# Nine instead of eight of 22 pairs by Strassen's products in the down projection of a decoder block, with repacked operands, per-phase pools and delayed first loads

## The chip, the core and the metric

The kernel runs on one core of one Trainium2 chip. The core has a matrix engine (TensorE, PE in the profile), a vector engine (VectorE, DVE), a scalar engine (ScalarE, ACT), GpSimd (POOL) and SyncE (SP), which here issues nearly all transfers. Each engine has its own instruction stream, and engines wait for one another by semaphores. The metric is the time of one launch on the device in microseconds; lower is better.

## The reference

One layer of a decoder block, on 256 tokens of width 2048, in float32:

```
proj = x @ w_in                      # q, k, v, gates of two mixers
y_gla = gated linear attention -> @ w_branch_gla
y_fox = forgetting attention   -> @ w_branch_fox
x = layer_norm(ALPHA*x + (sigmoid(ma)*y_gla + sigmoid(mb)*y_fox) @ w_out)
h = gelu(causal_dwconv(x @ w_gate)) * (x @ w_up)     # 256 x 5632
x = layer_norm(ALPHA*x + h @ w_down)                 # the down projection
x = x + sigmoid(x @ w_ple_gate) * (p @ w_ple_proj)   # the last stage
```

The change concerns above all `h @ w_down`, a product of 256 x 5632 by 5632 x 2048, and on the side the start (the values `fv` of forgetting attention), the turn into the MLP after the first LayerNorm, and the last stage.

## The kernel before, in words

**Precision.** Every float32 operand is split in two parts of a shorter format: `hi`, a copy by ScalarE (helper `copy`, L84), and `lo = value - hi`, by VectorE (L150). A product is three matmuls, hi by hi, hi by lo and lo by hi, added up in a PSUM bank.

**Weights.** The weights lie in memory as units of 128 x 2048, in the order in which they are used. `prep` (L137) loads a unit in two halves of 128 x 1024 on SP's queue into `raw` (5 buffers), and splits each half into `hi` and `lo` (6 buffers each). `unit` (L156) hands out the next unit and prepares up to two units ahead. SP's stream has the order in which the program was written; ScalarE's and VectorE's orders are made by a scheduler; TensorE's order is as written in some stretches (the ends of the two LayerNorm stages).

**Stages in order of time:** `fv` (4 to 54 us) in eight units of weights of 128 x 2096 (`fv_prep` L325, matmuls L358), the other projections, the mixers, the output projection `wo` with the first LayerNorm (767 to 875), gate and up (`psg`, `psu`, until 1358.8), the down projection in two halves of 1024 columns, `dn0` (1358.8 to 1476) and `dn1` (to 1593), the second LayerNorm, and the last stage `pg0` and `pg1` (1599 to 1692) with its results (`ev_o`, L1208 to L1219). The program ends at 1697.2.

**The down projection.** The 5632 rows of `w_down` make 44 tiles of 128, taken as 22 pairs. For a pair and a half of the columns, 256 tokens by 256 rows by 1024 columns is a 2 x 2 by 2 x 2 block product. A classic pair does the eight block products, three matmuls of 512 columns each (`classic`, L1075, 24 matmuls). A Strassen pair does seven block products on sums and differences of blocks (`strassen`, L1085, matmuls at L1071, 21 matmuls); `fold` adds the extra banks into the result. `DN_S` names the pairs done so, `DN_ORDER` their order in each half. The sums of the left operand are made once, in gate and up, by `sums` (L964), for the pairs in `DN_Y` not before all gate and up matmuls are issued. The differences of the weights are made for every unit by `prep_s` (L115): it loads two halves, takes four differences `T` of 512 columns (L132) and splits seven operands, the 512-column pieces by `pair512` (L104, low parts at L111), one half whole (L126).

**Left operands** lie in tiles `hC` (two classic pairs' hi and lo) and `hS` (the seven operands of a Strassen pair). Small work tiles of 512 columns come from `t2` (L74): six buffers in the pool `sm`, for the whole kernel; the differences, the `sums`, `tho` and `res` of the last stage are among them.

**First LayerNorm.** `end1` (L878) transposes the normalised rows in four column groups per 128 tokens (`turn0`, `turn1`, PE L789) and weaves them into the first matmuls of gate and up: `phase0` does the first 128 tokens of three banks, `phase1(j)` the second 128 tokens of column group j (24 matmuls of 256 columns). `turn1(G[3])` comes behind `phase1(0)`. `begin2` (L1169) does the like for the second LayerNorm and `pg0`.

**The last stage.** `ev_o` takes a bank of 128 x 512: ScalarE's tanh into `tho`, VectorE's product into `tho` (L1215) and sum into `res` (L1217), and a store by SP (L1219).

**The start.** The first transfers on SP are the activations `xraw` (`load_x`, L166) and the `fv` weights `fvraw`. Unit 0 comes in three chunks per half; then units 1, the next activations and unit 2 are issued as soon as buffers allow.

Of the kernel before, what the change touches and what calls it, by code (L numbers as in the profile page):

```python
# [19 lines left out]
P = 128  # L20
# [12 lines left out]
NS = 1048  # L33
# [8 lines left out]
DN_ORDER = ((0, 1, 2, 4, 3, 6, 5, 9, 7, 8, 11, 10, 14, 12, 16, 13, 19, 15, 17, 18, 20, 21),  # L42
            (0, 1, 2, 4, 3, 6, 5, 9, 7, 11, 8, 14, 10, 16, 12, 19, 13, 15, 17, 18, 20, 21))
# [10 lines left out]
def tile_block(ctx: ExitStack, tc: tile.TileContext, wu, wfv, wpp, xT_in, x_in, pT_in, wlr,  # L54
# [7 lines left out]
    early = ctx.enter_context(ExitStack())  # L62
    ec = early.enter_context(tc.tile_pool(name="ec", bufs=1))
    pmm = ctx.enter_context(tc.tile_pool(name="pmm", bufs=6, space=PSUM))
# [9 lines left out]
    def t2(name):  # L74
        return sm.tile([P, 512], F32, tag="t2", bufs=6, name=name)
# [28 lines left out]
    def pair512(a, b, name):  # L104

        hi, lo = [ring.tile([P, 1024], F32R, tag=t, name=f"{t}{name}") for t in ("hi", "lo")]
        out = []
        for src, e in ((a, slice(0, 512)), (b, slice(512, 1024))):
            if src is not None:
                copy(hi[:, e], src)  # L110
                nc.vector.tensor_tensor(lo[:, e], src, hi[:, e].bitcast(F32), ALU.subtract)  # L111
                out.append((hi[:, e], lo[:, e]))
        return out

    def prep_s(u):  # L115

        r0, r1 = [ring.tile([P, 1024], F32, tag="raw", bufs=5, name=f"raw{u}_{h}")
                  for h in range(2)]
        for h, r in enumerate((r0, r1)):
            nc.sync.dma_start(r, wu[u, :, h * 1024:(h + 1) * 1024])  # L120
        b12, b11, b22, b21 = r0[:, 0:512], r0[:, 512:1024], r1[:, 0:512], r1[:, 512:1024]
        ops = pair512(b11, None, f"b11_{u}")
        hi = ring.tile([P, 1024], F32R, tag="hi", name=f"hi{u}_1")
        copy(hi, r1)
        lo = ring.tile([P, 1024], F32R, tag="lo", name=f"lo{u}_1")
        nc.vector.tensor_tensor(lo, r1, hi.bitcast(F32), ALU.subtract)  # L126
        ops += [(hi[:, 512:1024], lo[:, 512:1024]), (hi[:, 0:512], lo[:, 0:512])]
        ts = {}
        for n, a, b in (("T1", b12, b11), ("T3", b12, b22), ("T2", b22, "T1"),
                        ("T4", b21, "T2")):  # L130
            ts[n] = t2(f"{n}_{u}")
            nc.vector.tensor_tensor(ts[n], a, ts.get(b, b) if isinstance(b, str) else b,  # L132
                                    ALU.subtract)
        ops += pair512(ts["T1"], ts["T3"], f"t13_{u}") + pair512(ts["T2"], ts["T4"], f"t24_{u}")
        ready[u] = ops
# [203 lines left out]

    load_x(0, 0, 1, 1)  # L340
    f0 = fv_prep(0, (0,))
    load_x(0, 1, 2, 1)
# [3 lines left out]
    load_x(1, 0, 4)  # L346
    for u in range(8):
        hi, lo = fvu[u]
        for j in range(2):
            kt = 2 * u + j  # L350
            a = xT[kt // 4][:, kt % 4, :]
            for cs in ((0,), (1,), (2,)) if u == 0 else ((0, 1, 2),):
                for t in range(2):
                    ah, al = a[:, t * P:t * P + P], a[:, 256 + t * P:256 + t * P + P]
                    for i, (w, x) in enumerate(((hi[j], ah), (lo[j], ah), (hi[j], al))):
                        for c in cs:
                            o, n = fch[c]
                            nc.tensor.matmul(fbk[t][c][:, 0:n], lhsT=x, rhs=w[:, o:o + n],  # L358
                                             start=kt == 0 and i == 0,
                                             stop=kt == 15 and i == 2)  # L360
# [207 lines left out]
    def a_gen():  # L568
        it = 0
        for h in range(H):  # L570
# [8 lines left out]
            phl = sm.tile([P, 2, 2, P], F32R, tag="t2", bufs=6, name="phl")  # L579
# [74 lines left out]
    def o_gen():  # L654
        parts, ogs = {}, {}

        def split(h):
            vs = s8([P, 2, 2, 512], F32R, name=f"vs{h}")
            copy(vs[:, 0], vg[h][:, 0])
            nc.vector.tensor_tensor(vs[:, 1], vg[h][:, 0], vs[:, 0].bitcast(F32), ALU.subtract)  # L660
            ah, al = [sm.tile([P, 384], F32R, tag="t2", bufs=6, name=n) for n in ("ath", "atl")]
# [65 lines left out]
    late = ctx.enter_context(tc.tile_pool(name="late", bufs=1))  # L727

# [149 lines left out]
    def end1(tail_mm):  # L878
# [3 lines left out]
        with tc.manual_schedule(engines={mybir.EngineType.PE}):  # L882
# [76 lines left out]
    gp = [late.tile([P, 264], F32, name=f"gp{i}") for i in range(2)]  # L959
    for i in range(2):  # L960
        nc.gpsimd.memset(gp[i][:, 0:2], 0.0)
    hC, hS, hY, yps = {}, {}, [], {}

    def sums(y, pair):  # L964
# [3 lines left out]
        o = hS[pair] = s8([P, 7, 256], F32R, name=f"hS{pair}")  # L968
# [3 lines left out]
        for e, src in ((slice(0, 1), y[:, 0:1, 0:P]),  # L972
                       (slice(1, 3), y[:, 1, :].rearrange("p (t n) -> p t n", t=2)),
                       (slice(3, 7), v)):
            copy(o[:, e, 0:P], src)
            nc.vector.tensor_tensor(o[:, e, P:256], src, o[:, e, 0:P].bitcast(F32),
                                    ALU.subtract)
# [9 lines left out]
    for n in range(NF):  # L987
# [29 lines left out]
        else:  # L1017
            nc.vector.tensor_tensor(y, y, u, ALU.mult)
            i = DN_C.index(pair)
            if i % 2 == 0 and j == 0:  # L1020
                hC[i // 2] = (s8 if i < 12 else late.tile)([P, 4, 512], F32R,
                                                           name=f"hC{i // 2}")
            dst = hC[i // 2][:, i % 2 * 2 + j, :]
            copy(dst[:, 0:256], y)
            nc.vector.tensor_tensor(dst[:, 256:512], y, dst[:, 0:256].bitcast(F32),
                                    ALU.subtract)
        if n >= 4:
            pull(1)

    for pair in DN_Y:  # L1030
        sums(yps.pop(pair), pair)
# [19 lines left out]
    def down(nh, tail, mid):  # L1051
# [23 lines left out]
        def classic(pair, w, toks=(0, 1), cs=(0, 1)):  # L1075
            i = DN_C.index(pair)
            for j in range(2):
                a = hC[i // 2][:, i % 2 * 2 + j, :]
                for t in toks:
                    ah, al = a[:, t * P:t * P + P], a[:, 256 + t * P:256 + t * P + P]  # L1080
                    for x, v in ((ah, w[0][j]), (ah, w[1][j]), (al, w[0][j])):
                        for c in cs:
                            mm(C[t][c], x, v[:, c * 512:c * 512 + 512])

        def strassen(pair, ops):  # L1085
            for ps, i, (hi, lo) in zip(prods, left, ops):
                ah, al = hS[pair][:, i, 0:P], hS[pair][:, i, P:256]
# [154 lines left out]
def _dst(w):  # L1242

    out = []
    for nh in range(2):
        for n in DN_ORDER[nh]:
# [3 lines left out]
            out.append(np.concatenate([b[0][1], b[0][0], b[1][1], b[1][0]] if n in DN_S  # L1250
# [72 lines left out]
```

## Time and profile before

| what | us |
|---|---|
| median of three runs | 1697.54 (1697.37 to 1697.68) |
| profiled execution, its own time | 1699.05 |
| its span in the trace | 1697.2 |
| TensorE busy | 1688.2 |
| VectorE busy | 1179.8 |
| ScalarE busy | 862.0 |
| `dn0`, `dn1` | 117 each |
| down-projection matmul, start to start | 0.232 |
| VectorE, low part of 128 x 1024 (mean duration) | 1.223 |

The span is the time from the first to the last instruction in the trace; the profiled execution's own time is 1.85 us longer. A group's idle time is that of its engine just before it, and what ended it; idle time of an engine that isn't the bottleneck costs nothing. The profile models the ends of matmuls, so their rate is read from start to start.

### The profile page before, as it was taken

The page shows a single profiled execution, that of the slowest core. Times are in us where ns is not written, and L with a number is a line of the kernel's source. Part 1 is how long each engine was busy: PE and PEld are TensorE (multiplying, and loading weights), DVE is VectorE, ACT ScalarE, POOL GpSimd, SP SyncE. Part 2 cuts the span into 40 slices and gives each one's busy share as a digit, 9 for nine tenths or more (in the row PEclk, how much of TensorE's full clock was granted, in tenths as well). Part 3 has the DMA queues.
Part 4 walks back from the last instruction along what each step waited for, and adds up shares of the span by engine and source line. Part 5 has one row for each costly group of instructions (what it writes and reads, how often), then busy time and mean ns, then how long its engine had stood idle before and what let it go on. Part 6 is the DMA issues. An engine that isn't in the chain of part 4 may idle for free.

```text
span 1697.2 us, 23968 instructions
## 1 busy us (share of the span) xinstructions
PE 1688.2 (99%) x8987; PEld 1448.1 (85%) x8987; DVE 1179.8 (70%) x1758; ACT 862.0 (51%) x1263; POOL 36.8 (2%) x123
## 2 busy tenths in 40 slices
PE   9999999999999999999999999999999999999998
PEld 8988888888888888888888888888888888888787
DVE  6666658768756546774687777766666798789764
ACT  6645445445555544443465455544444565456443
POOL 0000000000000000000010000000000000000000
PEclk9999999999999999999999999999999999999999
DMA  8654455555555455557645665555555556677444
GB/s 325 230 183 166 162 185 175 175 178 175 178 175 172 164 186 190 190 188 286 219 159 199 214 211 187 187 193 189 187 186 187 192 180 208 201 271 242 156 164 166
DMA packets 91717, 330.24 MB, mean 195 GB/s; under 512 B 10264, under 2 KB 11936, under 8 KB 90448
## 3 DMA queue, kind: packets, MB, share of 16 engines
q1 hardware_dynamic: 90816, 324.51, 56.2%
q0 software_dynamic: 784, 4.20, 0.6%
q8 instruction: 70, 1.15, 0.3%
q14 instruction: 47, 0.39, 0.1%
HBM read 323.42 MB, written 5.25 MB: 194 GB/s over the span
## 4 chain that ended last, share of the span: by engine, by line
PE 98%; DVE 1%; DMA 0%; SPq 0%; POOL 0%; issue 0%; ACT 0%
PE dn L1071 11%; PE psu L214 9%; PE psg L214 9%; PE psm L214 7%; PE gr L258 5%; PE gv L258 5%; PE pg L258 5%; PE wo L258 5%; PE psu L216 5%; PE psg L216 5%; PE psm L216 4%; PE psa L214 3%; PE dn_p L1071 3%; PE fv L358 2%; PE psa L216 2%; PE psfq L214 2%
## 5 line engine op out<-in xcount | busy, mean ns | idle before, releaser
L150 DVE TENSOR_TENSOR lo<-raw,hi 128x1024 fp32r<-128x1024 f32 x536 | 654.1, 1223 | 395.0 <-ACT hi L84 393.9
L84 ACT ACTIVATE hi<-raw 128x1024 fp32r<-128x1024 f32 x552 | 583.8, 1060 | 668.0 <-issue 269.4
L214 PE MATMUL psu<-x1T,hi 128*128 128x512 f32 x688 | 242.3, 393 | 0.0
L214 PE MATMUL psg<-x1T,hi 128*128 128x512 f32 x672 | 236.7, 393 | 0.0
L216 PE MATMUL psu<-x1T,lo 128*128 128x256 f32 x688 | 192.8, 280 | 0.0
L216 PE MATMUL psg<-x1T,lo 128*128 128x256 f32 x672 | 188.4, 280 | 0.0
L214 PE MATMUL psm<-xT,hi 128*128 128x512 f32 x512 | 180.0, 395 | 0.0
L214 PEld LDWEIGHTS psu<-x1T,hi 128*128 128x128 f32 x688 | 129.1, 188 | 29.6
L214 PEld LDWEIGHTS psg<-x1T,hi 128*128 128x128 f32 x672 | 126.1, 188 | 28.9
L216 PE MATMUL psm<-xT,lo 128*128 128x256 f32 x512 | 143.3, 280 | 0.0
L216 PEld LDWEIGHTS psu<-x1T,lo 128*128 128x128 f32 x688 | 129.6, 188 | 0.0
L216 PEld LDWEIGHTS psg<-x1T,lo 128*128 128x128 f32 x672 | 126.6, 188 | 0.0
L1071 PE MATMUL dn<-hi,hC 128*128 128x512 f32 x448 | 126.2, 394 | 0.0
L214 PEld LDWEIGHTS psm<-xT,hi 128*128 128x128 f32 x512 | 96.2, 188 | 21.6
L1071 PEld LDWEIGHTS dn<-hi,hC 128*128 128x128 f32 x448 | 84.1, 188 | 19.7
L216 PEld LDWEIGHTS psm<-xT,lo 128*128 128x128 f32 x512 | 96.5, 188 | 0.2
L214 PE MATMUL psa<-oT,hi 128*128 128x512 f32 x256 | 90.1, 394 | 0.0
L258 PE MATMUL gv<-hi,xT 128*128 128x512 f32 x256 | 73.6, 399 | 0.0
L258 PE MATMUL gr<-hi,xT 128*128 128x512 f32 x256 | 73.4, 399 | 0.0
L216 PE MATMUL psa<-oT,lo 128*128 128x256 f32 x256 | 71.6, 280 | 0.0
L258 PE MATMUL wo<-hi,mT 128*128 128x512 f32 x256 | 71.6, 395 | 0.0
L1071 PE MATMUL dn<-lo,hC 128*128 128x512 f32 x224 | 71.5, 394 | 0.0
(283 smaller groups left out, 2778.1 us busy)
## 6 DMA issues: line engine op xcount, KB each, us to landing
raw<-in_wu_dram SPq DMA_DIRECT2D x568, 512.0 KB, 3.7
fvraw<-in_wfv_dram SPq DMA_DIRECT2D x14, 524.0 KB, 6.8
lnb<-in_lng_dram SPq DMA_DIRECT2D x4, 1024.0 KB, 9.7
z<-in_x_dram SPq DMA_DIRECT2D x2, 1024.0 KB, 7.6
praw<-in_wpp_dram SPq DMA_DIRECT2D x4, 512.0 KB, 5.4
x1d<-z POOLq DMA_DIRECT2D x2, 1024.0 KB, 6.6
z<-x1d SPq DMA_DIRECT2D x4, 512.0 KB, 5.8
xraw<-in_xT_dram SPq DMA_DIRECT2D x7, 256.0 KB, 6.2
```

Source lines behind the costliest of these rows:

```text
L84: return nc.scalar.activation(o, i, AF.Copy, bias=0.0, scale=scale)
L150: nc.vector.tensor_tensor(lo, raw, hi.bitcast(F32), ALU.subtract)
L214: nc.tensor.matmul(ps, lhsT=hi[i // 8 if hoff == 0 else 0][:, w0 % 1024:w0 % 1024 + P], rhs=a[:, kt % 4, :], start=first and i == 0, stop= ...
L216: nc.tensor.matmul(ps[:, 256:512], lhsT=lo[i // 8 if hoff == 0 else 0][:, w0 % 1024:w0 % 1024 + P], rhs=a[:, kt % 4, 0:256], start=False, ...
L258: nc.tensor.matmul(bs[j][:, 0:m], lhsT=x, rhs=v[:, o:o + m], start=first and i == 0, stop=last and i == 2)
L358: nc.tensor.matmul(fbk[t][c][:, 0:n], lhsT=x, rhs=w[:, o:o + n], start=kt == 0 and i == 0, stop=kt == 15 and i == 2)
L1071: nc.tensor.matmul(ps, lhsT=x, rhs=w, start=todo[id(ps)] == total[id(ps)], stop=todo[id(ps)] == 1)
```

## The change

- **One more Strassen pair**: nine of 22 instead of eight, in both halves, with another order. In `dn0` the Strassen units stand at every second place from the third on (before, from the second); in `dn1` at places 2, 4, 6, 7, 9, 11, 12, 14 and 16 of 22, so that two times two of them are neighbours. The weights of a Strassen unit are laid out in the order b11, b22, b12, b21.
- **Cells**: the left operands lie in cells of 256 columns, eight to a tile (`cells`, `take`), instead of in `hC` and `hS`; a group of operands that crosses a tile is copied and subtracted in two pieces (`runs`).
- **Differences in pairs**: `prep_s` makes T1 and T3 with one subtraction of 1024 columns (one operand broadcast), and splits T1 with T3, T2 with T4, and b11 with b22 in 1024 columns. The difference tiles of 1024 columns (`T`) have two buffers.
- **Pools per phase**: `t2` takes its tiles from `ec`, then `md`, each with six buffers, and from the down projection on from `dnp` with three. `res` in the last stage takes half of a tile `T` of the two.
- **Turns**: `turn1(G[3])` comes behind `phase1(1)` instead of `phase1(0)`; `turns[1](1)` in `begin2` 12 matmuls later.
- **Start**: a tile `held` takes one of the five `raw` buffers until GpSimd has copied a column of the first weight half's low part into it, so that the third `fv` unit's first load waits for that; this load is issued ahead of the activations of the second group.

```diff
-DN_S = (1, 4, 6, 9, 11, 14, 16, 19)
-DN_Y = (11, 14, 16, 19)
+DN_S = (1, 3, 5, 8, 10, 12, 14, 16, 18)
+DN_Y = (12, 14, 16, 18)
...
-    def t2(name):
-        return sm.tile([P, 512], F32, tag="t2", bufs=6, name=name)
+    def t2(name, shape=(P, 512), dt=F32):
+        return scope[0].tile(list(shape), dt, tag="t2", bufs=6 if scope[0] is not dnp else 3,
+                             name=name)
...
-        b12, b11, b22, b21 = r0[:, 0:512], r0[:, 512:1024], r1[:, 0:512], r1[:, 512:1024]
-        ops = pair512(b11, None, f"b11_{u}")
...
-        for n, a, b in (("T1", b12, b11), ("T3", b12, b22), ("T2", b22, "T1"),
-                        ("T4", b21, "T2")):
-            ts[n] = t2(f"{n}_{u}")
...
-        ops += pair512(ts["T1"], ts["T3"], f"t13_{u}") + pair512(ts["T2"], ts["T4"], f"t24_{u}")
+        t13, t24 = [dnp.tile([P, 2, 512], F32, tag="T", bufs=2, name=f"T{u}_{i}")
+                    for i in range(2)]
+        sub = lambda o, a, b: nc.vector.tensor_tensor(o, a, b, ALU.subtract)
+        b11, b22 = split(r0, f"{u}_0")
+        b21, = split(r1[:, 1, :], f"{u}_1")
+        sub(t13, r1[:, 0:1, :].broadcast_to([P, 2, 512]), r0)
+        sub(t24[:, 0, :], r0[:, 1, :], t13[:, 0, :])
+        sub(t24[:, 1, :], r1[:, 1, :], t24[:, 0, :])
+        t1_, t3_ = split(t13, f"{u}_2")
+        t2_, t4_ = split(t24, f"{u}_3")
...
+    held = ring.tile([P, NS], F32, tag="raw", bufs=5, name="held")
     load_x(0, 0, 1, 1)
     f0 = fv_prep(0, (0,))
+    nc.gpsimd.tensor_copy(held[:, 0:1], f0[1][0][:, NS - 1:NS].bitcast(F32))
...
-    load_x(1, 0, 4)
     for u in range(8):
...
-        if u + 2 < 8:
+        if u == 0:
+            f2 = fv_prep(2, (0,))
+            load_x(1, 0, 4)
+            fvu.append(fv_prep(2, (1,), *f2))
+        elif u + 2 < 8:
...
                 phase1(j)
-                if j == 0:
+                if j == 1:
                     turn1(G[3])
...
-            i = DN_C.index(pair)
-            if i % 2 == 0 and j == 0:
-                hC[i // 2] = (s8 if i < 12 else late.tile)([P, 4, 512], F32R,
-                                                           name=f"hC{i // 2}")
...
+            hi, lo = [h[:, c, :] for h, c in take(used[0] + 2)]
+            hC[n] = hi, lo
+            copy(hi, y)
+            nc.vector.tensor_tensor(lo, y, hi.bitcast(F32), ALU.subtract)
...
-                    if t == 0 and i == 0:
+                    if t == 0 and i == 1:
                         turns[1](1)
...
             th = t2("tho")
-            r = t2("res")
+            r = dnp.tile([P, 2, 512], F32, tag="T", bufs=2, name="res")[:, 0, :]
```

More of the change, by code (lines that the diff above doesn't have):

```diff
@@ L102, in tile_block, with split @@
     ready = {}
[L104 to L113, printed above, removed]
+    def split(src, name):
+        n = src.shape[1] if len(src.shape) == 3 else 1
+        hi, lo = [ring.tile([P, 2, 512], F32R, tag=t, name=f"{t}{name}") for t in ("hi", "lo")]
+        h, l = (hi, lo) if n == 2 else (hi[:, 0, :], lo[:, 0, :])
+        copy(h, src)
+        nc.vector.tensor_tensor(l, src, h.bitcast(F32), ALU.subtract)
+        return [(hi[:, i, :], lo[:, i, :]) for i in range(n)]
@@ L956, in tile_block, with take, runs @@
     tc.keep_in_program_order(nc.scalar.preload_act_table_set("gelu_apprx_tanh_and_others"))
-    gp = [late.tile([P, 264], F32, name=f"gp{i}") for i in range(2)]
+    gp = [scope[0].tile([P, 264], F32, name=f"gp{i}") for i in range(2)]
     for i in range(2):
         nc.gpsimd.memset(gp[i][:, 0:2], 0.0)
-    hC, hS, hY, yps = {}, {}, [], {}
+    hC, hS, hY, yps, cells = {}, {}, [], {}, []
+    def take(n):
+        while len(cells) < n:
+            k = len(cells) // 8
+            new = (late.tile if k == NCELL else s8)([P, 8, 256], F32R, name=f"cells{k}")
+            cells.extend((new, c) for c in range(8))
+        out = cells[used[0]:n]
+        used[0] = n
+        return out
+    used = [0]
+    def runs(e, key):
+        out = []
+        for i in e:
+            if out and key(out[-1][-1]) is key(i):
+                out[-1].append(i)
+            else:
+                out.append([i])
+        return out
     def sums(y, pair):
```

64 lines of the change are left out of this document (32 added, 32 removed).

## The prediction, made before the changed kernel was timed

> **What bounds the kernel now.** I read the page first, then TensorE's waits, then the granted clock in stretches of the start, then the stages that the change touches in the timeline.
>
> ```profile
> PE 1688.2 (99%) x8987; PEld 1448.1 (85%) x8987; DVE 1179.8 (70%) x1758; ACT 862.0 (51%) x1263; POOL 36.8 (2%) x123
> ...
> PE 98%; DVE 1%; DMA 0%; SPq 0%; POOL 0%; issue 0%; ACT 0%
> ```
>
> TensorE works for 1688.2 of 1697.2 us and holds 98% of the chain that ended last. A change can gain only by fewer matmuls, by removing one of TensorE's few waits, or by a higher granted clock. It loses by a new wait.
>
> ```profile
> PE fv L358 <- ACT fvhi L84: 1.5, 1, 1.5
> PE warm_ps L94 <- DVE warm L91: 1.2, 1, 1.2
> PE ptl L789 <- issue: 0.6, 1, 0.6
> PE ptl L789 <- DVE lny L801: 0.4, 1, 0.4
> PE psg L227 <- DVE x1T L804: 0.2, 1, 0.2
> ```
>
> That is all of TensorE's waiting (total, times, longest): the second weight unit of FoX's values at the start, the first memset, and the transposes of the two LayerNorms. None is in the down projection. The granted clock around the first wait (stretch and length in us, busy time and instructions of TensorE, its weight loads, VectorE, ScalarE and GpSimd; then the granted clock, DMA share and GB/s):
>
> ```profile
> 10.70:14.10 3.40, 1.83 (x10) 1.43 (x10) 1.74 (x2) 2.68 (x4) 0.00 (x0) 1.00 1.03 413
> 14.10:17.50 3.40, 3.40 (x14) 3.40 (x13) 3.28 (x5) 2.68 (x4) 0.00 (x0) 0.50 1.03 419
> 17.50:21.00 3.50, 3.50 (x23) 3.50 (x23) 3.29 (x3) 3.06 (x4) 0.00 (x0) 0.99 1.03 411
> ```
>
> After the wait TensorE ran 3.4 us at half clock, worth 1.7 us; wait and slow stretch cost about 1.5 + 1.7 = 3.2 us. From 17.5 on the clock is whole.
>
> **Strassen's ninth pair.** A pair by Strassen is seven products of three matmuls, 21; a classic pair is 24. One pair more in each half of the down projection removes 2 x 3 = 6 matmuls of 512 columns. The first half, with its matmuls alone:
>
> ```profile
> 1358.80:1475.80 117.00, 117.00 (x505) 94.61 (x506) 1.00 0.61 204
> ```
>
> 8 x 21 + 14 x 24 = 504 matmuls fill it (one of the 505 is cut by the edge): 0.232 us each, no idle time. The gain is 6 x 0.232 = 1.4 us, provided that VectorE keeps up.
>
> **VectorE's work for a Strassen unit.** Its rate, first unit, before:
>
> ```profile
> 1368.90 0.68 DVE L111 TENSOR_TENSOR lob<-raw,hib 128x512 fp32r<-128x512 f32 x1
> 1369.50 1.21 DVE L126 TENSOR_TENSOR lo<-raw,hi 128x1024 fp32r<-128x1024 f32 x1
> 1370.63 0.68 DVE L132 TENSOR_TENSOR T<-raw 128x512 f32<-128x512 f32 x1
> 1371.24 0.68 DVE L132 TENSOR_TENSOR T<-raw,raw 128x512 f32<-128x512 f32 x1
> ```
>
> Start to start, 512 columns take 0.605 us and 1024 take 1.13. Before, a unit is nine of 512 and one of 1024: 6.58 us. After, it is three of 512 (one low part, two differences) and four of 1024 (one difference with a broadcast operand, three low parts): 6.34 us. The broadcast has no row; I take a 1024-column subtraction, between 1.13 and two of 512, 1.21. A classic unit takes 2 x 1.13 = 2.26. A Strassen and a classic unit together need 8.6 us of VectorE and (21 + 24) x 0.232 = 10.4 of TensorE, so the two-buffer tiles of differences have 1.8 us a pair to hide ScalarE's copies between them. Where two Strassen units stand side by side (both only in the second half) TensorE takes 9.7 and VectorE 12.7; the three us missing come from the prefetch of two units. I count 0; bounds 0 to 5.4 (0.3 us late at each of 18 units, half of ScalarE's 0.61 us for a 512-column copy).
>
> At the entry VectorE works without a pause from 1355.5 to 1368 on the last sums; the first Strassen unit moves from second to third place. TensorE reaches it at 1358.8 + 48 x 0.232 = 1369.9 and needs the low part of its first difference nine matmuls on, at 1372.0; adding VectorE's steps in the new order behind its last sum (low parts to 1367.6, differences to 1369.9, low part to 1371.1) leaves 0.9 us. 0; bounds 0 to 1. The extra `sums` call and its copies into cells lie in gate/up, where VectorE is 70% busy and TensorE waits for nothing: 0, bounds 0 to 0.5.
>
> **Results through two buffers.** Here I find a loss. The results `res` of the last stage used six buffers and now use the two of the differences, so the third result waits until the first has landed in memory, and the fourth for the second. Before, in the timeline, with the summary row of the output transfers:
>
> ```profile
> 1647.15 0.69 DVE L1217 SCALAR_TENSOR_TENSOR res<-tho,z 128x512 f32<-128x512 f32 x1
> ...
> 1647.87 4.32 SPq L1219 DMA_DIRECT2D out_dram<-res  x4
> ...
> 1651.14 0.69 DVE L1217 SCALAR_TENSOR_TENSOR res<-tho,z 128x512 f32<-128x512 f32 x1
> 1652.28 6.67 SPq L146 DMA_DIRECT2D raw<-in_wu_dram  x6
> 1656.28 1.06 ACT L84 ACTIVATE hi<-raw 128x1024 fp32r<-128x1024 f32 x1 [7.74 <-DMA raw<-in_wu_dram]
> 1657.37 1.23 DVE L150 TENSOR_TENSOR lo<-raw,hi 128x1024 fp32r<-128x1024 f32 x1 [5.54 <-ACT hi L84]
> DMA to landing us min/median/max: 1.9/2.2/3.3
> ```
>
> SP's queue is in order: the six weight loads stand behind the four stores. VectorE's new order is tho, tho, res, res, tho, tho, res, res. The first result ends about 1648.45 (0.6 later), the second about 1649.05. With the 3.3 us that the first store took before, the third result runs 1651.8 to 1652.5, the fourth to 1653.1, and the loads leave at 1653.6, 1.3 us late; with landings of 2.2 us they are 0.3 late. TensorE reaches that unit at 1658.44 and needs its low part two matmuls on, at 1658.9; it was ready at 1658.60. Of 1.3 us, 0.3 are covered: **+1.0**, bounds 0 (short landings) to 1.6. I take the long landing because it is this very store's row.
>
> In the tail:
>
> ```profile
> 1691.48 2.41 SPq L1219 DMA_DIRECT2D out_dram<-res  x3
> ...
> 1693.11 0.42 DVE L1217 SCALAR_TENSOR_TENSOR res<-tho,z 128x256 f32<-128x256 f32 x1
> ```
>
> The last result, at 1693.11, now waits for the store issued at 1691.48; the trace has it landed at 1693.70 (2.2 us). Nothing is left to cover it: **+0.6**, bounds 0.3 (landing in 1.9) to 0.8.
>
> **Turns moved later.** The last transposes of the first LayerNorm's second half (874.54 to 874.89 before) go behind 24 more matmuls of 256 columns (2.8 us at 0.117), to 877.35. In the new order ScalarE does three weight halves ahead of the turned columns and VectorE their low parts. The third half overwrites one that the matmuls before the turn read until 877.5: ScalarE's copy 1.05 after that, VectorE's low part 1.22, its low part of the columns 0.69, and some 0.05 for each hand-over, give 880.6. TensorE wants the columns at 880.43: **+0.2**, bounds 0 to 1. The 0.4 and 0.2 us waits of that stretch end by 871.6, ahead of the move, and stay. In the second LayerNorm one turn goes behind 12 matmuls of 512 columns; the 0.6 us there belongs to an earlier turn (1600.24), which stays: 0, bounds -0.3 to 0.3.
>
> **First loads held back.** The third unit's first load now waits for a GpSimd copy and precedes four activation loads. The late unit is the second: its load is issued at 4.97, unchanged and ahead of all that is moved, landed at 11.18, and ScalarE's copy (1.08 us) ran from 11.20, TensorE from 12.33. Loads land in the order issued (11.18, 12.48, 13.14, 13.77, 15.02), so I see no competition to remove: 0. The third unit was ready at 17.4 and wanted at 20.08; a hold to about 6.0 doesn't reach it. Bounds: -3.2 (wait and slow clock both go) to +1.5 (the wait doubles).
>
> **Sum.** -1.4 + 1.0 + 0.6 + 0.2 = +0.4 us. The profiled execution took 1699.05 us, 1.5 over the median of the runs (1697.54), so 1699.45 in its own time and **1697.9** against the median: no measurable change, a bound that I set at 0.2%, 3.4 us.
>
> The Trainium skill, "TensorE: Matmul & The Clock Gate", Part 1, says that the clock falls to half after a whole window of some 3.4 us of idleness. This trace disagrees: a 1.5 us wait was followed by 3.4 us at 0.50. By the page the 1.0 us wait at 1659 could not slow the clock and the sum stays; by the trace a wait a little longer might, for 1.7 us more, 1699.6.
>
> **Rivals.** (A) *The start is cured.* If transfers in flight share the memory's rate after all, holding the others back brings the second unit 1.5 us sooner and the half-clock stretch goes too: 1697.9 - 3.2 = 1694.7; without the new store waits (-1.6) 1693.1. For it: this load took 2.65 us behind the one before it, the next equal one 1.3. Against: the order of landing. Chance 0.22, of which two thirds fall below 1694.1.
>
> (B) *Lateness in the differences* (slower). Difference tiles with two buffers tie a unit's VectorE steps to the low parts of the unit before. If each of the 18 units comes 0.3 us late, TensorE waits 5.4 us in all: 1703.3; it passes 0.2% (1700.9) from 0.17 us a unit. Against: 1.8 us of slack a pair; for: VectorE enters saturated and the second half has neighbours. Chance 0.2.
>
> (C) *Only the saving shows*: stores land quickly and the turn is covered, 1697.54 - 1.4 = 1696.1, up to 1696.7 with the tail's wait alone. Chance 0.15, within 0.2%.
>
> **How the numbers follow.** Forecast 0.43, A 0.22, B 0.20, C 0.15. Faster takes two thirds of A and a little of C: 0.16. Slower takes most of B and the forecast's upper bounds (1.6 + 0.8 + 1.0 - 1.4, with 1.7 for a second slow stretch: +3.7): 0.2. The rest, 0.64, is the same. The range runs from most of A, 1693.5, to most of B, 1702.5; the forecast's own is 1696.7 to 1699.6.
>
> **What would show it.** In the changed profile: 9 x 21 + 13 x 24 = 501 matmuls in each half without idle time between them; in the waits a line of pg for the late weights (1.0) and results waiting for stores at 1651 and 1693; fv's wait of 1.5 and the 0.50 stretch still there. I am wrong if dn appears among the waits, if fv's wait has gone, or if the half-clock stretch comes a second time.

## The result, and the profile after

The changed kernel takes 1703.25 us on the median of eight runs (1701.71 to 1705.03), the kernel before 1697.55 us (1696.83 to 1699.64): the ratio is 1.0033, with an interval of 1.0023 to 1.0042. It is slower by 5.7 us, more than the 3.4 us (0.2%) that the prediction took as its bound for no measurable change, and lies 0.75 us above the predicted range. The profiled execution of after took 1705.03 us, 1.8 over its median; that of before was 1.5 over its own.

The page and TensorE's waits of the kernel after (total, times, longest):

```profile
span 1702.9 us, 23927 instructions
...
PE 1690.1 (99%) x8981; PEld 1446.9 (85%) x8981; DVE 1185.7 (70%) x1729; ACT 861.0 (51%) x1240; POOL 37.6 (2%) x124
```
```profile
PE pg L259 <- ACT hi L90: 1.6, 1, 1.6
PE warm_ps L100 <- DVE warm L97: 1.2, 1, 1.2
PE dn L1104 <- DVE lo L151: 1.1, 1, 1.1
PE fv L362 <- ACT fvhi L90: 1.0, 1, 1.0
PE ptl L798 <- issue: 0.6, 1, 0.6
PE pg L259 <- DVE lo L151: 0.5, 1, 0.5
PE ptl L798 <- DVE lny L810: 0.4, 1, 0.4
PE psg L228 <- DVE x1T L813: 0.2, 1, 0.2
```

New are two waits of the last stage (`pg`), as forecast but larger, and one in the down projection (`dn`), which the prediction had put at nothing and had named as a sign of being wrong. Six matmuls fewer, yet 1.9 us more of busy time: in the last stage alone it rose by 2.1 us (92.3 to 94.4), a second effect of the `pg` waits. In the stretches of the last stage, each 3.41 us, busy time of TensorE comes after the length, and the granted clock third from the end:

```profile
1655.25:1658.67 3.42, 3.42 (x21) 2.97 (x20) 0.00 (x0) 0.00 (x0) 0.00 (x0) 1.00 0.78 223
1658.67:1662.08 3.41, 1.29 (x6) 0.60 (x5) 1.23 (x1) 1.99 (x2) 0.00 (x0) 1.00 1.00 371
1662.08:1665.49 3.41, 3.41 (x10) 2.85 (x11) 2.78 (x3) 2.38 (x4) 0.00 (x0) 0.50 0.99 396
1665.49:1668.90 3.41, 3.41 (x20) 2.98 (x20) 3.10 (x3) 1.99 (x2) 0.00 (x0) 1.00 0.83 263
```

TensorE stood still for most of the second stretch and ran the third at half clock, 10 matmuls instead of 20: 1.7 us lost. The half-clock stretch that the start of before had (14.12 to 17.54) is absent.

From the first matmul of each stage to that of the next, in us of the two traces:

| stretch | before | after | difference |
|---|---|---|---|
| start to the first matmul after `fv` (`smp`) | 54.56 | 53.41 | -1.16 |
| to the first `psu` | 810.81 | 811.41 | +0.60 |
| gate and up | 493.39 | 494.56 | +1.17 |
| down projection and second LayerNorm | 240.55 | 240.34 | -0.21 |
| last stage, to TensorE's end | 92.88 | 97.14 | +4.26 |
| TensorE's end to the end | 4.97 | 6.07 | +1.10 |

Most of the loss is in the last stage. VectorE's results and SP's queue there, after:

```profile
1648.20 1.29 DVE L1249 SCALAR_TENSOR_TENSOR res<-tho,z 128x512 f32<-128x512 f32 x2
1649.41 1.28 DVE L1247 SCALAR_TENSOR_TENSOR tho<-tho,ppk 128x512 f32<-128x512 f32 x2
1651.26 0.69 DVE L1249 SCALAR_TENSOR_TENSOR res<-tho,z 128x512 f32<-128x512 f32 x1 [0.57 <-DMA out_dram<-res]
1654.16 0.69 DVE L1249 SCALAR_TENSOR_TENSOR res<-tho,z 128x512 f32<-128x512 f32 x1 [2.21 <-DMA out_dram<-res]
```
```profile
1648.91 6.30 SPq L1251 DMA_DIRECT2D out_dram<-res  x4
1655.31 6.98 SPq L147 DMA_DIRECT2D raw<-in_wu_dram  x6
```

The third result waits for the first store (0.57 us), the fourth for the second (2.21 us), and the weight loads behind the four stores leave at 1655.31, 5.8 us after `pg1`'s first bank starts; before, it was 3.3 (1652.28 against 1648.95). The first store landed as a whole 2.26 us after its issue. Of the second, issued at 1649.52, fifteen of sixteen parts had landed by 1651.88 and the last at 1654.07. In the tail the last result waited too:

```profile
1697.32 0.42 DVE L1247 SCALAR_TENSOR_TENSOR tho<-tho,ppk 128x256 f32<-128x256 f32 x1 [0.42 <-ACT tho L1246]
1699.23 0.43 DVE L1249 SCALAR_TENSOR_TENSOR res<-tho,z 128x256 f32<-128x256 f32 x1 [1.49 <-DMA out_dram<-res]
```

### The profile page after: what moved, and what is told of

Read it like the earlier page. It is cut to its first block, busy times and chain, and to the rows that moved or that the text cites. A ratio compares the mean times of both kernels' runs of the same rounds, so it can differ in the third digit from the quotient of the medians.

```text
span 1702.9 us, 23927 instructions
## 1 busy us (share of the span) xinstructions
PE 1690.1 (99%) x8981; PEld 1446.9 (85%) x8981; DVE 1185.7 (70%) x1729; ACT 861.0 (51%) x1240; POOL 37.6 (2%) x124
## 4 chain that ended last, share of the span: by engine, by line
PE 91%; DVE 5%; DMA 2%; issue 1%; ACT 1%; SPq 0%; POOL 0%; DVEq 0%; ACTq 0%
PE psu L215 9%; PE psg L215 9%; PE psm L215 7%; PE dn L1104 7%; PE gv L259 5%; PE gr L259 5%; PE wo L259 5%; PE psu L217 5%; PE psg L217 5%; PE pg L259 4%; PE psm L217 4%; PE psa L215 3%; PE fv L362 2%; PE psa L217 2%; PE psfq L215 2%; PE psq L215 2%
## 5 line engine op out<-in xcount | busy, mean ns | idle before, releaser
L90 ACT ACTIVATE hi<-raw 128x1024 fp32r<-128x1024 f32 (+1 forms) x568 | 591.0, 1045 | 652.3 <-issue 259.1
L1104 PE MATMUL dn<-hi,cells 128*128 128x512 f32 x524 | 154.6, 394 | 0.0
L1104 PEld LDWEIGHTS dn<-hi,cells 128*128 128x128 f32 x524 | 98.3, 188 | 23.1
L1104 PE MATMUL dn<-lo,cells 128*128 128x512 f32 x262 | 87.8, 394 | 1.1 <-DVE lo L151 1.1
L259 PE MATMUL pg<-hi,x2T 128*128 128x512 f32 (+1 forms) x256 | 71.2, 386 | 1.6 <-ACT hi L90 1.6
```

Of the source, the lines that this page charges most:

```text
L90: return nc.scalar.activation(o, i, AF.Copy, bias=0.0, scale=scale)
L259: nc.tensor.matmul(bs[j][:, 0:m], lhsT=x, rhs=v[:, o:o + m], start=first and i == 0, stop=last and i == 2)
L1104: nc.tensor.matmul(ps, lhsT=x, rhs=w, start=todo[id(ps)] == total[id(ps)], stop=todo[id(ps)] == 1)
```

## The experiments

The median of the kernel before in the same comparisons was 1697.6 to 1697.7.

### Results with places of their own

```diff
     for nh in range(2):
+        rs = s8([P, 4, 512], name=f"res{nh}")
...
-            r = dnp.tile([P, 2, 512], F32, tag="T", bufs=2, name="res")[:, 0, :]
+            r = rs[:, 2 * t + c, :]
```

> The changed kernel with a separate place for each of the nine results, so that no result waits for a store. Theory (the two-buffer results cost the last stage a late weight load, a half-clock window and a late last store): TensorE's pauses of 1.75, 0.70 and 0.29 us at 1659 to 1662 go, the clock stays whole after them (1.7), the last result no longer waits 1.5 us; about 5.5 us less than the changed kernel, 1697.5 to 1698.5, pg1 back at 43.3 us between its last-bank start and TensorE's end. Rival (the late loads come from a slow transfer and not from the result buffers): the pauses stay and the time stays above 1701.

Measured: 1700.03 us (1697.50 to 1702.04, 11 runs), 1.0014 of before, 1.0005 to 1.0023. No result waits, `pg` keeps one pause of 0.5 us, no half-clock stretch follows. The last stage took 93.56 us and the tail 4.62: in the traces 3.6 and 1.45 us less than after. The median fell by 3.2 us, not 5.5. The pause in `dn` is still there, but the changed kernel's trace has it too, so it explains none of the difference; that not every execution of the changed kernel pays for the half clock is likely, but not shown. The two buffers of the results are the largest part of the loss.

### Two places for the results, alone, in the kernel before

```diff
+    rs, n_res = s8([P, 2, 512], name="res"), [0]
     for nh in range(2):
...
-            r = t2("res")
+            r = rs[:, n_res[0] % 2, :]
+            n_res[0] += 1
```

> The kernel before, with its results alone put through two places in turn and nothing else changed. Theory: this alone costs what the last stage lost, 3 to 5.5 us: 1700.5 to 1703, with the loads after the four stores issued 1 to 3 us later and the third and fourth result waiting for stores. If the late part of a store is a 16th part held up by an instruction fetch, the size depends on where that fetch falls, and without one in the way the loss is 1 to 2 us. Rival (the pool change or the rest of the change is needed for the loss): 1697.5, no change.

Measured: 1699.40 us (1698.96 to 1700.09, 11 runs), 1.0011 of before, 1.0002 to 1.0019: 1.75 us. In the trace the last stage takes 93.92 us (+1.04) and the tail 5.75 (+0.78). So the results alone cost here what the prediction had worked out, 1.0 and 0.6, and not what they cost in the changed kernel. The expected 3 to 5.5 us did not come. Something in the changed kernel makes the same wait longer.

### An instruction fetch moved

A trace shows 70 transfers of 16 KB of the instruction queue, each of about 1 us, for 18000 instructions of TensorE (loads and matmuls): one per 256 on average. In after one runs from 1651.45 to 1652.41, in the second store; before, from 1648.78 to 1649.94, in the first, whose last part also came late (15 parts by 1650.06, the last at 1651.21) but kept nobody waiting. The profile doesn't name the DMA engine of a transfer; that the late part stood behind the fetch on one engine is inferred from the times: in after the fetch ends at 1652.41, and the next 2 KB packet of any transfer starts at 1652.40. This run moves the fetch.

```diff
-    for _ in range(9):
-        nc.tensor.matmul(pw_, lhsT=warm[:, 0:P], rhs=warm, start=True, stop=True)
+    for n in [512] * 4 + [8] * 20:
+        nc.tensor.matmul(pw_[:, 0:n], lhsT=warm[:, 0:P], rhs=warm[:, 0:n], start=True, stop=True)
```

> The changed kernel with five of the nine warming matmuls at the very start replaced by twenty of 8 columns, about as long together, so that TensorE's instruction stream is 30 instructions longer before everything else and each 16 KB instruction fetch (one per 256 TensorE instructions) falls some 3.5 us earlier in the work. Theory (the fourth result waits for the one part of the second store that queues behind such a fetch on its DMA engine): the fetch near the stores now falls before the second store's data, that store lands within 2.5 us, the fourth result starts before 1652.7, the weight loads leave about 2 us earlier than in the changed kernel, at most 1.2 us of pauses are left in pg and no half-clock window follows: 2 to 4 us less than the changed kernel in the profile, 1700.5 to 1702 on the median. Rival (the store is slow for its place in the kernel, not for the fetch): its last part still comes 2 us behind the other fifteen, and the time is that of the changed kernel.

Measured: 1700.65 us (1698.89 to 1703.49, 11 runs), 1.0018 of before, 1.0009 to 1.0028, and 2.6 less than the changed kernel. VectorE and SP in its trace:

```profile
1650.30 1.48 DVE L1249 SCALAR_TENSOR_TENSOR res<-tho,z 128x512 f32<-128x512 f32 x2 [1.01 <-DMA out_dram<-res]
```
```profile
1647.52 4.63 SPq L1251 DMA_DIRECT2D out_dram<-res  x4
1652.23 10.19 SPq L147 DMA_DIRECT2D raw<-in_wu_dram  x8
```

The fetch now ran at 1647.78 to 1648.74, in the first store. The second store landed whole in 2.9 us, the fourth result ran in one go with the third, the loads left 4.1 us after `pg1`'s first bank starts (1652.23 against 1648.12; after: 5.8), and one pause of 0.69 us was left, with no half clock behind it. Nothing in the program of the last stage had changed but where the fetch fell. The pause in `dn` was shorter too in this trace (0.5 us against 1.1), so the 2.6 us are not all the fetch's. The other traces agree: of all thirteen, in the eight in which a fetch runs in the second store, that store's last part lands 2.1 to 2.5 us after the other fifteen; in the five in which it runs in the first, the first store's last part is 0.3 to 1.7 us late. With places of their own the late part is there as well (1653.41 after 1651.29), and no result waits for it. So the long wait of after takes both, results in two buffers and a store with a fetch in it.

### Pauses put into TensorE's work

```diff
+        k = {8: 0, 11: 0, 14: 1, 17: 1, 20: 1, 23: 2, 26: 2, 29: 3, 32: 3, 35: 4}.get(n)
+        if k is not None:
...
+                z = psg
+                for i in range(k):
+                    z_ = t1("pz")
+                    copy(z_, z[:, 0:256])
+                    z = z_
+                zr = t1("pzr").bitcast(F32R)
+                copy(zr[:, 0:P], z[:, 0:P])
+                mx = mxtile(f"pause{n}")
+                nc.tensor.matmul(mx[:, 0:P], lhsT=zr[:, 0:P], rhs=zr[:, 0:P], start=True, stop=True)
```

> The kernel before with ten pauses of TensorE put into gate and up, one each 33 us: a small matmul waits for a chain of zero to four ScalarE copies of the bank just finished. Theory (the clock is judged in fixed windows of 3.413 us, and a window in which TensorE stood still for 1.5 us or more, one number between 1.43 and 1.62, is followed by one at half clock; shorter idleness is not): each half-clock stretch of the trace is one window long, starts a whole number of windows after the others, and follows a window with more than 1.43 us of idleness; pauses of more than 1.6 us that fall on both sides of a window's edge are not followed by one. Rival (any pause of more than some 1.5 us slows the clock, wherever it falls): every pause above 1.6 us is followed by one.

Measured: 1762.03 us, one execution. The pauses came out at 3.1 to 5.1 us, longer than meant, so nothing near 1.5 us was tried; each was followed by half clock. Every half-clock stretch of all traces begins a whole number of 3.413 us after the first full-clock record. But seven of the ten stretches of this run last two windows, not one as expected:

```profile
1001.68:1005.10 3.42, 2.91 (x9) 2.53 (x10) 1.54 (x4) 0.69 (x2) 0.37 (x2) 0.50 0.53 171
1005.10:1008.51 3.41, 3.41 (x13) 2.93 (x12) 0.00 (x0) 0.80 (x1) 0.00 (x0) 0.50 0.02 5
```

The first windows of these seven were busy for 1.5 to 2.9 us and the clock stayed at half; it came back after windows that were busy for 3.26 us or more. What follows is therefore said of windows that begin at full clock. With the grid the other runs bound the rule there. Windows along it, of the kernel before, of the run with the later pairs (next section), of the run with the old start (the one after that) and of the two-place run; each pair is the window with the pause and the one behind it:

```profile
10.71:14.12 3.41, 1.84 (x10) 1.45 (x10) 1.76 (x2) 2.70 (x4) 0.00 (x0) 1.00 1.04 417
14.12:17.54 3.42, 3.42 (x14) 3.42 (x13) 3.30 (x5) 2.66 (x3) 0.00 (x0) 0.50 1.01 413
```
```profile
1655.43:1658.84 3.41, 2.16 (x12) 1.73 (x12) 0.31 (x1) 1.06 (x1) 0.00 (x0) 1.00 1.00 322
1658.84:1662.25 3.41, 2.89 (x16) 2.14 (x16) 2.86 (x3) 2.65 (x3) 0.00 (x0) 1.00 1.01 411
```
```profile
1654.91:1658.32 3.41, 2.02 (x12) 1.59 (x10) 0.00 (x0) 0.72 (x1) 0.00 (x0) 1.00 0.88 265
1658.32:1661.74 3.42, 2.50 (x11) 1.80 (x12) 2.45 (x2) 2.45 (x3) 0.00 (x0) 1.00 1.02 406
```
```profile
11.17:14.58 3.41, 2.06 (x11) 1.77 (x12) 2.33 (x3) 3.04 (x4) 0.00 (x0) 1.00 1.03 415
14.58:18.00 3.42, 3.42 (x23) 3.42 (x22) 3.28 (x5) 2.47 (x4) 0.00 (x0) 1.00 1.02 418
```

A window with 1.84 us of busy time (before) or 1.29 (after, above) is followed by one at 0.50; windows with 2.02, 2.06 and 2.16 are not. The old-start run's pause of 1.94 us, counted from when the next matmul was due, is longer than the 1.67 us of before, yet a window's edge cuts it and the clock stays. At the ends of the two kernels of "The parts undone together" a window with 1.91 and one with 1.88 us are not followed by half clock either. So a window at full clock that is busy less than some 1.84 to 1.88 of its 3.41 us halves the next, and whether one pause does depends on where the grid falls in that execution. The rival is out: a pause of over 1.6 us alone does not do it.

### The last five Strassen pairs one place later

```diff
-DN_ORDER = ((0, 2, 1, 4, 3, 6, 5, 7, 8, 9, 10, 11, 12, 13, 14, 15, 16, 17, 18, 19, 20, 21),
+DN_ORDER = ((0, 2, 1, 4, 3, 6, 5, 7, 8, 9, 11, 10, 13, 12, 15, 14, 17, 16, 19, 18, 20, 21),
```

> The changed kernel with one more classic pair after the fourth Strassen pair of the first half, so that the last five stand one place later. Theory (with a Strassen unit at every second place the loads of a Strassen unit are issued 11.9 us apart while TensorE uses 10.4 us a pair, so the lead is eaten until the ninth is late): the 1.3 us pause at 1448.8 goes, 1.3 us less than the changed kernel, about 1702. Rival (an instruction fetch or a single slow transfer made it): the pause stays or moves by one pair, no change.

Measured: 1703.38 us (1700.85 to 1706.03, 5 runs), 1.0033 of before, 1.0021 to 1.0046. The median shows no gain over the changed kernel; runs that spread over 5 us cannot show 1.3. The trace does: no `dn` wait is left, and the down projection takes 238.98 us against 240.34. What made the pause, in the trace of after, by SP, VectorE and TensorE (L124 loads a Strassen unit, L147 a classic one):

```profile
1428.35 1.46 SPq L124 DMA_DIRECT2D raw<-in_wu_dram  x2
1430.09 8.71 SPq L147 DMA_DIRECT2D raw<-in_wu_dram  x2
1440.21 1.46 SPq L124 DMA_DIRECT2D raw<-in_wu_dram  x2
```
```profile
1447.17 1.23 DVE L128 TENSOR_TENSOR T<-raw,raw 128x1024 f32<-128x1024 f32 x1 [2.99 <-DMA raw<-in_wu_dram]
1448.43 0.69 DVE L128 TENSOR_TENSOR T<-raw,T 128x512 f32<-128x512 f32 x1
1449.05 1.22 DVE L151 TENSOR_TENSOR lo<-raw,hi 128x1024 fp32r<-128x1024 f32 x1
```
```profile
1450.32 0.73 PE L1104 MATMUL dn<-lo,cells 128*128 128x512 f32 x2 [1.12 <-DVE lo L151]
```

VectorE is idle for 3 us, waiting for the ninth Strassen unit's load, while the classic unit's low part, which TensorE needs first, stands behind that difference in its stream. The load is late because a Strassen unit's loads wait for raw buffers that the classic unit's low parts free. This circle took 9.0 to 11.3 us for the earlier units and 12.4 and 11.9 for the last two (loads at 1415.97, 1428.35 and 1440.21); TensorE needs 10.4 for the pair. So the lead shrinks by 1.5 to 2 us in each of the last turns until the ninth unit is late. With two classic units in between, it recovers. The other traces with the order of after pause there too, for 0.5 to 1.1 us.

### The start of the kernel before in the changed kernel

```diff
-    held = ring.tile([P, NS], F32, tag="raw", bufs=5, name="held")
...
-    nc.gpsimd.tensor_copy(held[:, 0:1], f0[1][0][:, NS - 1:NS].bitcast(F32))
...
+    load_x(1, 0, 4)
     for u in range(8):
...
-        if u == 0:
-            f2 = fv_prep(2, (0,))
-            load_x(1, 0, 4)
-            fvu.append(fv_prep(2, (1,), *f2))
-        elif u + 2 < 8:
+        if u + 2 < 8:
```

> The changed kernel with the start of the kernel before (no held buffer, third unit's load not held back). Theory (the start gained 1.2 us because the pause of the second unit, 1.2 us, stayed below what sets the clock to half in a window of 3.4 us): 1 to 3 us slower than the changed kernel, 1704 to 1706, with a half-clock window between 10 and 21 us when the pause grows to 1.6. Rival (the start's gain comes from where the clock's windows fall in that execution, not from the order of the loads): no difference on the median, within 0.5 us of the changed kernel.

Measured: 1702.78 us (1701.50 to 1703.79, 6 runs), 1.0032 of before, 1.0019 to 1.0044: 0.5 less than the changed kernel, not 1 to 3 more. The theory fell. `fv` ends at 53.28 us without the hold, 53.41 with it; and in the two-place run, whose start is that of the kernel before, at 53.15 with whole clock. The 1.2 us by which after leads at the start were the half-clock stretch in this one execution of before, not the order of the loads. The wait of `fv` itself was shorter with the hold, 0.5 to 1.0 us in the six traces that have it against 1.1 to 1.7 in the seven others, but in both groups `fv` ends between 52.8 and 53.5 us wherever the clock was whole. And something else moved: gate and up, 800 us away, takes 493.62 us again instead of 494.56.

### The hold alone, and the held buffer without the hold

The first run puts the start of the changed kernel into the kernel before (the lines above the other way round, here its core). The second keeps all of the changed kernel but releases the held buffer at once.

```diff
+    held = ring.tile([P, NS], F32, tag="raw", bufs=5, name="held")
...
+    nc.gpsimd.tensor_copy(held[:, 0:1], f0[1][0][:, NS - 1:NS].bitcast(F32))
```
```diff
-    nc.gpsimd.tensor_copy(held[:, 0:1], f0[1][0][:, NS - 1:NS].bitcast(F32))
+    nc.gpsimd.memset(held[:, 0:1], 0.0)
```

> The kernel before with the held buffer and the late third load alone. Theory of addresses (holding a buffer changes which hi and lo buffers a unit's two halves get for the rest of the program, and with the second set of addresses a 512-column matmul of gate and up takes 232.45 instead of 231.35 ns): gate and up from the first psu matmul to the first dn matmul 494.5 us instead of 493.4, some 1.9 us in all, 1699 to 1699.7 where the kernel before has 1697.65. Rival (the slower matmuls come from the new pools and cells of the changed kernel): gate and up stay at 493.4 and the time at 1697.3 to 1698.

> The changed kernel, the held buffer released at once (a memset instead of the copy of split weights), the order of the first loads kept as changed. Its hi and lo buffers have the addresses of the kernel before, its raw buffers those of neither. Theory of addresses: gate and up 493.4 to 493.7 us, 1.9 us gained before the down projection, 1701 to 1703.5 as with the old start. Rival (the order of the first loads, or the raw buffers, make the matmuls slower): 494.5 us.

Measured: the hold alone 1698.35 us (1697.84 to 1699.09, 11 runs), 1.0004 of before, 0.9995 to 1.0013; the changed kernel with the buffer released 1701.62 us (1699.73 to 1702.51, 10 runs), 1.0022 of before, 1.0013 to 1.0031. Gate and up takes 494.29 us in the first and 493.61 in the second. The row of the first `psu` matmuls and that of `dn`, before, after, hold alone, buffer released (first and last start after the durations):

```profile
L227 PE MATMUL psu<-x1T,hi x32: 277/280/363, 865.4 to 882.3; 128*128 128x256 f32 x32
...
L1071 PE MATMUL dn<-hi,hC x448: 387/394/402, 1358.8 to 1592.6; 128*128 128x512 f32 x150
```
```profile
L228 PE MATMUL psu<-x1T,hi x32: 278/280/366, 864.8 to 882.0; 128*128 128x256 f32 x32
...
L1104 PE MATMUL dn<-hi,cells x524: 387/394/400, 1359.4 to 1593.1; 128*128 128x512 f32 x175
```
```profile
L227 PE MATMUL psu<-x1T,hi x32: 277/281/366, 864.7 to 881.6; 128*128 128x256 f32 x32
...
L1076 PE MATMUL dn<-hi,hC x448: 387/394/401, 1359.0 to 1592.7; 128*128 128x512 f32 x150
```
```profile
L228 PE MATMUL psu<-x1T,hi x32: 277/280/363, 863.8 to 881.0; 128*128 128x256 f32 x32
...
L1104 PE MATMUL dn<-hi,cells x524: 387/394/401, 1357.4 to 1590.7; 128*128 128x512 f32 x175
```

The hold, and not the pools or cells, makes gate and up 0.9 to 1.0 us longer; with 0.5 between `fv` and `psu` it is 1.4, in the first run as in the second. Holding one raw buffer for a moment changes the order in which later buffers come free, and with it which `hi` and `lo` buffer most later units have. In the buffer layouts of the programs, before, the run with the old start and the released buffer give every half the same `hi` and `lo` buffer up to the down projection, and so do after and the hold alone with each other; the raw buffers of the released run agree with neither. With the first assignment a 512-column matmul of gate and up starts 231.4 ns after the one before, with the second 232.3 to 232.5. The places repeat every three units. One unit in three has the same `hi` and `lo` buffers in both assignments and takes 5599 ns in both; the other two take 5616 and 5558 ns in the first and 5628 and 5579 in the second, to 1 ns the same in all kernels of one assignment. The 85 units that run whole take 475.25 us in before and 476.19 in after and in the hold alone.

The rest of the 1.17 us is the moved turn of the first LayerNorm. In after, by VectorE and TensorE:

```profile
879.50 0.68 DVE L717 TENSOR_TENSOR x1T<-ptl,x1T 128x512 fp32r<-128x512 f32 x1
```
```profile
879.96 0.28 PE L232 MATMUL psg<-x1T,lo 128*128 128x256 f32 x1
880.25 0.39 PE L228 MATMUL psg<-x1T,hi 128*128 128x256 f32 x1
880.47 0.28 PE L232 MATMUL psg<-x1T,lo 128*128 128x256 f32 x1
```

The matmul at 880.25 starts 0.29 us after the one before it, when the turned columns' low part is ready at 880.18, and the next 0.22 later; the rest stand 0.12 apart. This delay, 0.24 us or more, is in every trace with the moved turn and in none without; the list of waits doesn't show it, because the matmul before is counted as busy until 880.24.

The hold alone cost only 0.7 us on the median and lies within its interval of nothing, so the loss is shown in the stretches and not in the time. Its down projection was 0.3 us shorter than before (240.28), which takes part of the 1.4 back.

### Separate rings for first and second halves

A third assignment, on the last kernel of the next section: each `hi` and `lo` half takes its buffer from a ring of three of its own (one of the lines).

```diff
-            hi = ring.tile([P, 1024], F32R, tag="hi", name=f"hi{u}_{h}")
+            hi = ring.tile([P, 1024], F32R, tag=f"hi{h}", bufs=3, name=f"hi{u}_{h}")
```

> The kernel with separate places for the results, the later place of the last five Strassen pairs and the old start, with the hi and lo buffers of first and second halves in separate rings of three. Theory of addresses: a third set of addresses gives a third length of gate and up, apart from 493.6 and from 494.5 by more than 0.2 us, the same for all units of one buffer; the sign is open, the time 1695.5 to 1699. Rival (addresses don't matter, only which buffer comes free when): gate and up within 0.1 us of 493.6.

Measured: 1698.37 us (1696.42 to 1702.02, 11 runs), 1.0005 of before, 0.9996 to 1.0014. Gate and up takes 494.21 us, but that is not the units alone: the matmul behind the moved turn waits 0.58 us here. The 85 whole units take 475.45 us, 5594, 5638 and 5549 ns in turn: a third length, 0.2 us from the first. The rings also bind the order: `dn` waits 2.6 us at 1454 and a half-clock window follows, so the time says nothing of the addresses. That a unit's length goes with the places of its `hi` and `lo` buffers is shown by these three assignments, and by the units that keep their buffers and their length; why it does, and which accesses collide, was not tried.

### The parts undone together

The first run has the edits of "Results with places of their own" and "The last five Strassen pairs one place later" together, the second in addition that of "The start of the kernel before":

```diff
+        rs = s8([P, 4, 512], name=f"res{nh}")
...
+DN_ORDER = ((0, 2, 1, 4, 3, 6, 5, 7, 8, 9, 11, 10, 13, 12, 15, 14, 17, 16, 19, 18, 20, 21),
```

> The changed kernel with separate places for the results and the later place of the last five Strassen pairs. Theory: the pauses at 1449 and 1659 are gone (0.5 us at most left in pg), what is left against the kernel before is the slower matmul (+1.9) and the gain of six matmuls (-1.4): 1698.0 to 1699.0, and with no pause over 1.4 us outside the start the spread of the runs falls to some 2 us. Rival (the spread of the runs has another cause than pauses that set the clock to half): 1697.5 to 1702 as with separate places alone.

> As the run before it, with the start of the kernel before in addition, so that the hi and lo buffers are those of the kernel before. Theory: gate and up at 493.5 us, dn0 and dn1 together at 239.0 against 240.55, pg as with separate places: 1696.5 to 1697.2, below the kernel before by 0.5 to 1.1 us. Rival (the cells or the pools cost something of their own): 1697.6 or more.

Measured: 1698.77 us (1697.93 to 1701.20, 11 runs), 1.0008 of before, 0.9999 to 1.0017; and with the old start 1697.22 us (1696.58 to 1700.21, 11 runs), 0.9999 of before, 0.9990 to 1.0008. Three edits take the changed kernel from +5.7 to -0.5 us, which can't be told from nothing. In the trace the last one's down projection takes 239.37 us, 1.2 less than before: nine Strassen pairs, cells and pools show no cost of their own beyond the 0.25 us of the moved turn. The spread did not fall to 2 us; pauses at the start remain, and why it is not smaller stays open.

## Why the prediction was wrong, point by point

Three terms failed. "Results through two buffers" was mis-sized, 1.0 us where the last stage lost 4.3, because the 3.3 us landing was taken as the first store's own and the half clock that a longer wait brings stood outside the sum. "VectorE's work for a Strassen unit" was put at 0 by comparing busy times, and cost 1.3 us. "First loads held back" was put at 0 because only the start was looked at, and cost 1.4 us later. Rival B's 1703.3 us lies beside the measured 1703.25 by chance: its mechanism gave 1.3 of its 5.4 us.

- **Six matmuls, -1.4: right.** Without a pause the down projection takes 238.98 or 239.37 us against 240.55, -1.6 or -1.2.
- **VectorE's work, 0: wrong.** The step compared 8.6 us of VectorE's busy time with 10.4 of TensorE's. The circle of load, difference, low parts and free buffer took 12.4 and 11.9 in its last two turns and was not counted. It cost 1.3 us, once, not 0.3 at each of 18 units as rival B had it; the entry, put at 0, was right.
- **Results through two buffers, +1.0: right in mechanism, wrong in size.** The waits came as worked out, third result behind the first store, fourth behind the second, loads behind both. In the kernel before this costs 1.04 us. In the changed kernel the fourth result ran at 1654.16 instead of 1652.5: the step took the 3.3 us of one store for that very store's own, when they came with an instruction fetch, which in the changed kernel falls in the second store. In all 2.7 us of pauses came (counted from when the next matmul was due), and 1.7 of half clock.
- **The tail, +0.6:** it measured 1.1 in after, 0.8 alone. The store that the last result waits for landed its last part 3.0 us after issue, not 2.2.
- **The clock.** The prediction had a second slow stretch only as an upper bound. The traces show half clock after windows at full clock that were busy for 1.84 and 1.29 of 3.41 us, and none after 1.88 or more. That stretch is 1.7 of the 1705.03 us of the profiled execution. The Trainium skill, "TensorE: Matmul & The Clock Gate", Part 1, wants a whole window of idleness. These traces disagree, with 1.84 us of busy time in the window.
- **Turns, +0.2 and 0: right.** The turned columns were late as worked out, and TensorE lost some 0.25 us to them. The listed LayerNorm waits are 0.6, 0.4 and 0.2 us in both kernels.
- **First loads, 0: right on the time at the start, wrong on the whole.** Rival A did not pay: the wait of `fv` became shorter, yet `fv` ends no earlier with the hold than without. The cost lay where the prediction didn't look, +1.4 us of stretches that go with the places of the buffers.

The sum of what the runs showed, in the traces: -1.6 for the matmuls, +1.3 for the pause in `dn`, +2.7 and +1.7 in the last stage, +1.1 in the tail, +1.4 for the buffers' places and +0.25 for the turn, or 6.9. Between the traces it was 5.8, mostly because the trace of before holds a half-clock stretch at the start, 1.4 us, that the two-place run with the same start doesn't have.

## What to carry to other kernels

When a pool gets fewer buffers, ask what releases each of them: where it is a store, the wait lasts until the slowest of its parts has landed, and an instruction fetch can make one part late. Compare TensorE's time with the whole circle that frees a buffer (load, steps, release), not with the busy time of the engine that feeds it. Compare also the length of stages that the change doesn't touch: a buffer held for a moment can give most later tiles another place.

## What the runs showed of the hardware

- TensorE's granted clock changes on a grid of 3.413 us that is fixed within an execution. A window at full clock that was busy for 1.84 us or less was followed by one at 0.50, one with 1.88 or more was not; a window already at 0.50 and busy for 1.5 to 2.9 us was followed by another, one busy for 3.26 us or more was not. A half-clock window costs 1.7 us of work.
- TensorE's instructions come in 16 KB transfers of about 1 us, one per 256 instructions on average (27 to 32 us apart in the down projection). In the last stage of thirteen traces a store of 256 KB with such a transfer in it landed its last part 0.3 to 2.5 us after the other fifteen.
- The same 512-column matmuls ran 0.4 to 0.5% slower in gate and up with another assignment of weight buffers (232.3 to 232.5 against 231.4 ns), 800 us after the edit that caused it.
